# A fused transformer block on one core: constants made by another engine, a product 4 ticks sooner

## The chip, the cores and the metric

The kernel runs on one core of a Trainium2 chip. The core has a matrix engine (TensorE, PE in the rows), a vector engine (VectorE, DVE), an activation engine (ScalarE, ACT), a general engine (GpSimd, POOL) and a queue engine that issues most transfers (SyncE, SP). Each runs its own instructions in the order in which they were written and waits on semaphores for the others. The metric is the device time of one execution in microseconds (us), lower is better.

## The reference

One layer for 256 tokens of width 1024, in float32. `norm` is the root-mean-square norm over a row with a gain:

```python
h = norm(x, norm_mix_g);  proj = h @ w_in                  # u | q | k | v, 512 columns each
q, k = rope(norm_per_head(q)), rope(norm_per_head(k))      # 8 heads of 64
attn = causal_softmax(q @ k.T / 8) @ v
pool = (window_means(u, 2, 4, 8, 16) - u) @ pool_w * pool_scale   # 4 groups of 128
x = x + concat(pool, attn) @ w_out
h, m = norm(x, norm_xattn_g), norm(mem, norm_mem_g)        # mem: 256 x 1024
x = x + cross_attention(h @ w_xq, m @ w_xkv) @ w_xo        # 4 heads of 256, q and k normed
h = norm(x, norm_ffn_g)
up = causal_conv3(h @ w_up) + conv_b                       # 5632 columns: gate | val
x = x + (silu(gate) * val) @ w_down
```

The sequence is one block of 256 positions, so the attention over selected blocks comes to plain causal attention.

## The kernel before, in words

Weights stream from memory in chunks of 1 MB, each two units of 128x1024. Three buffers hold raw chunks (tile `raw`). For every unit ScalarE rounds it to a short format (`wh`, line 194) and VectorE makes what the rounding lost (`wl`, line 205); a product is then three matmuls: high by high, low by high, high by low. A raw buffer takes its next chunk only when both of its units have been through both engines. `need(u)` issues these two steps some units ahead of the one that TensorE takes up.

The order of work is written out by hand. TensorE's main work is a chain of matrix products. `a_chunk` computes 256 rows by 512 columns in eight steps of six 512-column matmuls (lines 366, 367 and 370) over units `u0` to `u0+3`. The first four calls make k, q, v and u (units 0 to 15, two steps a unit). Units 16 and 17 are one chunk of small constants for the pool mixing. Units 18 to 25 serve the keys of the memory, and the output projection follows, tile by tile (`b_tile`, lines 265 to 267).

Everything else is done by jobs, Python generators that each issue a few instructions and then yield. `tick()` lets every living job go one yield further; `a_chunk` calls it twice a step. So four ticks are two steps, and the tables `WAIT_...` say how many ticks a job lets pass at each of its places. Since every engine works in order, these numbers fix the order on each queue, not only the earliest time. `finish(jobs)` calls `tick` until the jobs named have ended.

These jobs matter here:

- `row_stat("x")` computes the mean square of each row of x. ScalarE makes eight squares (the first into `accx`, line 297, the others `sqx`, line 300), GpSimd adds them up (seven adds, line 301), then `WAIT_STAT[1]` ticks pass, and TensorE multiplies `accx` by a column of ones (line 281). VectorE makes `vx` of it (284), GpSimd `ex` (289). The same function with "m" serves the memory rows, and it reads the same `WAIT_STAT[1]`.
- `rope_table` makes the rotary tables `ropek` and `ropeq` on GpSimd (line 382), out of `tab`, a table that a transfer brings.
- `qk_job("k")` rotates k on VectorE: `m1k` out of `ropek` (404), `m2k` (408), the sums of squares `ssk` (411) and `m1k` again (413). Then it waits until `ex` has been issued, makes the head scale (`hk` at line 243, `rs1y` at 226, then twelve small GpSimd steps, lines 228 to 231), scales `m1k` by it (431), and TensorE transposes it (438). ScalarE copies the result to `qkT` (442). `qk_job("q")` does the same for q with `m1q` and `m2q`, and its scale ends in `sp` and `sneg` (445, 446).
- `score_job` (attention) takes the maximum of the scores, `nbs` from it and `sneg` (530), and the exponentials.
- `late_constants` makes `identr` and the first part of `maskr` (387, 388), which the scores need (515).
- `pool_job` splits u into `uh` and `ul` (250, 256), mixes (621 to 624), multiplies by the pool weights and empties the two banks into `cat` (643). `WAIT_POOL[7]` is the wait after that, at its end (644).

Of the kernel before, what the change touches and what calls it, by code (L numbers as in the profile page):

```python
# [16 lines left out]
P = 128  # L17
# [20 lines left out]
FIRST = 4  # L38

WAIT_MEAN = [0]  # L40
WAIT_STAT = [2, 14, 8, 0, 0, 30]
WAIT_ROPE = [6, 6, 0]
WAIT_QK = [12, 12, 8, 25, 0, 2]
WAIT_V = [2, 10]
WAIT_MEM = [2, 2]
WAIT_SCORE = [5, 4, 0, 9, 1, 6]
WAIT_ATTN = [2, 6, 0]
WAIT_POOL = [1, 6, 0, 7, 1, 5, 2, 6, 1]
WAIT_KEY = [0, 4, 7, 2, 0, 13, 5]
WAIT_R1 = [0]  # L50
WAIT_X = [3, 0, 0, 0, 10, 0, 6, 13, 8]
# [17 lines left out]
T_ID, T_MASK = 0, 128  # L69
T_COS, T_SIN = 384, 512  # L70
T_GQ, T_GQS, T_GK, T_GKS = 640, 704, 768, 832
# [5 lines left out]
def block_kernel(ctx: ExitStack, tc: tile.TileContext, wpack: bass.AP, xpack: bass.AP, scal: bass.AP,  # L77
                 memT: bass.AP, table: bass.AP, out: bass.AP):
    nc = tc.nc
    pe, act, dve, pool = nc.tensor, nc.scalar, nc.vector, nc.gpsimd  # L80
# [15 lines left out]
    def t2(name, dtype=F32):  # L96
        return temps.tile([P, 512], dtype, name=name, tag="t2", bufs=19)

    def t1(name):
        return temps.tile([P, S], F32, name=name, tag="t1", bufs=8)  # L100
# [12 lines left out]
    def go(gen):  # L113

        job = [gen, True]
        jobs.append(job)
        step(job)
        return job
# [16 lines left out]
    def wait(n):  # L135
        for _ in range(n):
            yield
# [7 lines left out]
    resid = sc[:, C_X:C_X + KT * S].rearrange("p (k s) -> p k s", k=KT)  # L145
    tab = const.tile([P, T_COLS], F32, name="tab")
# [32 lines left out]
    maskr = const.tile([P, 6 * P], F32R, name="maskr")  # L179
# [42 lines left out]
    def rsqrt(x, n):  # L222

        cnt[0] += 1
        y, t = sm(f"rs{cnt[0]}y", n), sm(f"rs{cnt[0]}t", n)
        dve.tensor_scalar(y.bitcast(I32), x.bitcast(I32), -0.5, float(0x5F3759DF), op0=ALU.mult, op1=ALU.add)
        for _ in range(3):
            pool.tensor_tensor(t, y, y, op=ALU.mult)  # L228
            pool.tensor_tensor(t, t, x, op=ALU.mult)
            pool.tensor_scalar(t, t, -0.5, 1.5, op0=ALU.mult, op1=ALU.add)  # L230
            pool.tensor_tensor(y, t, y, op=ALU.mult)
        return y
# [13 lines left out]
    def part_h(h, src, scale=None):  # L246
        if scale is None:
            act.copy(h, src)
        else:
            act.activation(h, src, AF.Copy, scale=scale)  # L250

    def part_l(l, src, h, scale=None):
        if scale is None:
            dve.tensor_tensor(l, src, h.bitcast(F32), op=ALU.subtract)
        else:
            dve.scalar_tensor_tensor(l, src, scale, h.bitcast(F32), op0=ALU.mult, op1=ALU.subtract)  # L256
# [12 lines left out]
    def col(t, c):  # L269
        return t[:, c:c + 1]  # L270
# [6 lines left out]
    def row_mean(acc, name):  # L277

        b = bank()
        for tt in range(TT):  # L280
            pe.matmul(b[:, tt:tt + 1], acc[:, tt * P:(tt + 1) * P], ones, start=True, stop=True)
        yield from wait(WAIT_MEAN[0])
        v = sm("v" + name, TT)
        dve.tensor_scalar(v, b[:, 0:TT], 1.0 / D, EPS, op0=ALU.mult, op1=ALU.add)
        return v

    def times_eps(v, name):
        e = sm("e" + name, TT)
        pool.tensor_scalar(e, v, EPS, None, op0=ALU.mult)
        return e  # L290

    def row_stat(name, src, behind=None):
        yield from wait(WAIT_STAT[3 if name == "x" else 4])
        acc = t1("acc" + name)
        for k in range(KT):
            if k == 0:
                act.activation(acc, src(k), AF.Square)
            else:
                sq = t1(f"sq{name}{k}")
                act.activation(sq, src(k), AF.Square)  # L300
                pool.tensor_tensor(acc, sq, acc, op=ALU.add)
            yield from wait(WAIT_STAT[0])
        if behind:
            behind()
        yield from wait(WAIT_STAT[1])
        v = yield from row_mean(acc, name)
        rows["e" + name] = times_eps(v, name)
        yield from wait(WAIT_STAT[2 if name == "x" else 5])
        rows[name] = rsqrt(v, TT)
# [64 lines left out]
    ident = tab[:, T_ID:T_ID + P]  # L374
    identr = const.tile([P, P], F32R, name="identr")
# [3 lines left out]
    def rope_table(n, g, gs):  # L379
        t = const.tile([P, 2, TT, HD], F32, name="rope" + n)  # L380
        for j, (c, gg) in enumerate(((T_COS, g), (T_SIN, gs))):
            pool.tensor_tensor(t[:, j], tab[:, c:c + 2 * HD].rearrange("p (t d) -> p t d", t=TT),
                               tab[:, None, gg:gg + HD].to_broadcast([P, TT, HD]), op=ALU.mult)
        rope_t[n] = t

    def late_constants():
        pool.tensor_copy(identr, ident)
        pool.tensor_copy(maskr[:, 0:2 * P], tab[:, T_MASK:T_MASK + 2 * P])
        pool.tensor_tensor(ggx, sc[:, C_GXQ:C_GXQ + 2], sc[:, C_GXK:C_GXK + 2], op=ALU.mult)


# [59 lines left out]

    def stat_job():

        yield from row_stat("x", lambda k: resid[:, k], lambda: rope_table("q", T_GQ, T_GQS))
        late_constants()

    rope_table("k", T_GK, T_GKS)
    stat_x = go(stat_job())
    bk = [bank(), bank()]
    a_chunk(0, xgv, bk)  # L460
# [135 lines left out]
    def pool_job():  # L596
        yield from wait(WAIT_POOL[8])

        rct = [t2(f"rct{i}") for i in range(2)]
        for g, w in enumerate(WINDOWS):  # L600
            r = rct[g // 2][:, g % 2 * S:(g % 2 + 1) * S]
            pool.memset(r[:, 16:], 1.0 / w)
            pool.tensor_copy(r[:, 0:16], tab[:, T_CNT + 16 * g:T_CNT + 16 * g + 16])
        us = []
        for tt in range(TT):
            us.append((t2(f"uh{tt}", F32R), t2(f"ul{tt}", F32R)))
            part_h(us[tt][0], bu[tt], col(rows["x"], tt))
        yield from wait(WAIT_POOL[0])
        for tt in range(TT):
            part_l(us[tt][1], bu[tt], us[tt][0], col(rows["x"], tt))  # L610
        yield from wait(WAIT_POOL[1])
        bp = []
        for g2 in range(2):
            b = bank()
            for i in range(2):
                g = 2 * g2 + i
                o = b[:, i * S:(i + 1) * S].rearrange("p (a s) -> p a s", a=2)
                c = slice(g * P, (g + 1) * P)
                b0 = misc[g2][:, i * S:(i + 1) * S].rearrange("p (a s) -> p a s", a=2)
                b1 = maskr6[:, 0:g + 3:g + 2]  # L620
                pe.matmul(o, us[0][0][:, c], b0, start=True, stop=False)
                pe.matmul(o, us[0][1][:, c], b0, start=False, stop=False)
                pe.matmul(o, us[1][0][:, c], b1, start=False, stop=False)
                pe.matmul(o, us[1][1][:, c], b1, start=False, stop=True)
            yield from wait(WAIT_POOL[2])
            pf, ph, pl = t2(f"pf{g2}"), t2(f"poolh{g2}", F32R), t2(f"pooll{g2}", F32R)
            dve.tensor_tensor(pf, b, rct[g2], op=ALU.mult)
            yield from wait(WAIT_POOL[3])
            act.copy(ph, pf)
            yield from wait(WAIT_POOL[4])  # L630
            dve.tensor_tensor(pl, pf, ph.bitcast(F32), op=ALU.subtract)
            bp.append((ph, pl))
        yield from wait(WAIT_POOL[5])
        for g2 in range(2):
            b = bank()
            for i in range(2):
                g = 2 * g2 + i
                w = [misc[3][:, g * P:(g + 1) * P], misc["l"][:, g * P:(g + 1) * P]]
                three(b[:, i * S:(i + 1) * S], w, [t[:, i * S:(i + 1) * S] for t in bp[g2]], True, True)
            yield from wait(WAIT_POOL[6])  # L640
            for i in range(2):
                g = 2 * g2 + i
                evac_split(cat[0][:, g], cat[1][:, g], b[:, i * S:(i + 1) * S], col(sc, C_PS + g))
        yield from wait(WAIT_POOL[7])
# [402 lines left out]
```

## Time and profile before

| what | value |
|---|---|
| time, median of 3 runs | 394.69 us (394.58 to 394.85) |
| the profiled execution | 395.07 us |
| its span, first to last instruction | 393.3 us |
| PE busy | 387.0 us (98%) |
| DVE busy | 283.1 us (72%) |
| ACT busy | 231.5 us (59%) |
| POOL busy | 90.0 us (23%) |

The span leaves out 1.77 us of the execution's own time, before the first and after the last instruction. PE's busy share is near the whole span, so what delays PE in its order delays the end, unless PE would have had to wait later anyway.

### The profile page before, as it was taken

How to read it: one execution, taken by the hardware profiler on the slowest of the kernel's cores; microseconds unless marked ns; L12 is line 12 of the kernel's file. 1: busy time of each engine (PE TensorE's matmuls, PEld its weight loads, DVE VectorE, ACT ScalarE, POOL GpSimd, SP SyncE). 2: the span in 40 equal slices, each digit the busy share in tenths (PEclk: the TensorE clock that was granted, in tenths of full speed). 3: DMA queues.
4: the chain of work that ended last, by engine and by line, in shares of the span. 5: the costliest groups of instructions: out<-in, count | busy, mean ns of one | idle time of the engine just before them, and what ended most of it. 6: DMA issues, size and time to landing. Idle time of an engine off the chain costs nothing.

```text
span 393.3 us, 7301 instructions
## 1 busy us (share of the span) xinstructions
PE 387.0 (98%) x2898; PEld 367.2 (93%) x2898; DVE 283.1 (72%) x478; ACT 231.5 (59%) x421; POOL 90.0 (23%) x174
## 2 busy tenths in 40 slices
PE   8999999999999999999999999999999999999996
PEld 7878787889999998899999999999999999999996
DVE  4788989956876667857774999998877874543350
ACT  5775886957476556845555498765665576342300
POOL 0384883134441423001647300000000000000000
PEclk9999999999999999999999999999999999999999
DMA  8985372543336537242545226665465452455400
GB/s 273 422 342 207 119 304 72 166 190 108 109 107 222 208 107 262 76 198 107 202 143 197 105 108 227 243 249 177 176 213 180 161 197 108 135 227 176 173 21 19
DMA packets 12274, 69.22 MB, mean 176 GB/s; under 512 B 1360, under 2 KB 2768, under 8 KB 4688
## 3 DMA queue, kind: packets, MB, share of 16 engines
q1 hardware_dynamic: 11952, 68.24, 47.9%
q8 instruction: 22, 0.36, 0.4%
q10 hardware_dynamic: 288, 0.52, 0.4%
q14 instruction: 12, 0.10, 0.1%
HBM read 67.71 MB, written 1.05 MB: 175 GB/s over the span
## 4 chain that ended last, share of the span: by engine, by line
PE 80%; DVE 7%; DMA 5%; ACT 3%; POOL 2%; issue 2%; SPq 0%; DVEq 0%; POOLq 0%
PE bank L265 23%; PE bank L267 23%; PE bank L266 23%; DMA raw<-wpack 3%; PE bank L366 3%; PE bank L367 3%; PE bank L370 3%; DVE wl L205 2%; DMA sc<-xpack 1%; ACT wh L194 1%; DVE mg_l L256 1%; ACT sqx L300 0%; PE bank L677 0%; PE bank L795 0%; POOL rs3t L228 0%
## 5 line engine op out<-in xcount | busy, mean ns | idle before, releaser
L205 DVE TENSOR_TENSOR wl<-raw,wh 128x1024 fp32r<-128x1024 f32 (+1 forms) x126 | 150.3, 1209 | 5.4 <-ACT wh L194 5.3
L194 ACT CAST wh<-raw 128x1024 fp32r<-128x1024 f32 (+1 forms) x125 | 123.7, 1024 | 41.6 <-DMA raw<-wpack 41.0
L265 PE MATMUL bank<-hs_h,wh 128*128 128x256 f32 x288 | 81.5, 283 | 0.0
L266 PE MATMUL bank<-hs_l,wh 128*128 128x256 f32 x288 | 81.5, 283 | 0.0
L267 PE MATMUL bank<-hs_h,wl 128*128 128x256 f32 x288 | 81.5, 283 | 0.0
L265 PEld LDWEIGHTS bank<-hs_h,wh 128*128 128x128 f32 x288 | 55.3, 192 | 0.0
L266 PEld LDWEIGHTS bank<-hs_l,wh 128*128 128x128 f32 x288 | 55.3, 192 | 0.0
L267 PEld LDWEIGHTS bank<-hs_h,wl 128*128 128x128 f32 x288 | 55.3, 192 | 0.0
L265 PE MATMUL bank<-act_h,wh 128*128 128x256 f32 x176 | 49.8, 283 | 0.0
L266 PE MATMUL bank<-act_l,wh 128*128 128x256 f32 x176 | 49.8, 283 | 0.0
L267 PE MATMUL bank<-act_h,wl 128*128 128x256 f32 x176 | 49.8, 283 | 0.0
L903 DVE SCALAR_TENSOR_TENSOR y<-bank,sc,y 128x255 f32<-128x255 f32 (+1 forms) x72 | 29.8, 479 | 14.4 <-ACT y L896 14.4
L265 PE MATMUL bank<-h_h,wh 128*128 128x256 f32 x128 | 36.6, 286 | 0.0
L267 PE MATMUL bank<-h_h,wl 128*128 128x256 f32 x128 | 36.2, 283 | 0.0
L266 PE MATMUL bank<-h_l,wh 128*128 128x256 f32 x128 | 36.2, 283 | 0.0
L896 ACT ACTIVATE y<-bank,sc 128x256 f32<-128x256 f32 x36 | 18.3, 559 | 27.6 <-PE bank L267 27.6
L265 PEld LDWEIGHTS bank<-act_h,wh 128*128 128x128 f32 x176 | 33.8, 192 | 0.0
L266 PEld LDWEIGHTS bank<-act_l,wh 128*128 128x128 f32 x176 | 33.8, 192 | 0.0
L267 PEld LDWEIGHTS bank<-act_h,wl 128*128 128x128 f32 x176 | 33.8, 192 | 0.0
L946 DVE TENSOR_TENSOR o<-bank,sc 128x256 f32<-128x256 f32 x8 | 3.4, 425 | 35.2 <-PE bank L267 35.2
L366 PE MATMUL bank<-wh,mg_h 128*128 128x512 f32 x64 | 26.1, 408 | 0.0
L726 POOL TENSOR_TENSOR h_acc<-h_sq,h_acc 128x256 f32<-128x256 f32 x14 | 16.8, 1198 | 40.3 <-ACT h_sq L725 40.2
(244 smaller groups left out, 862.4 us busy)
## 6 DMA issues: line engine op xcount, KB each, us to landing
raw<-wpack SPq DMA_DIRECT2D x59, 1024.0 KB, 4.8
raw<-wpack SPq DMA_DIRECT2D x4, 512.0 KB, 7.7
mraw<-memT SPq DMA_DIRECT2D x4, 256.0 KB, 7.7
out<-o SPq DMA_DIRECT2D x8, 128.0 KB, 1.9
raw<-wpack ACTq DMA_DIRECT2D x2, 256.0 KB, 3.7
raw<-wpack SPq DMA_DIRECT2D x2, 256.0 KB, 4.7
sc<-xpack SPq DMA_DIRECT2D x1, 512.0 KB, 6.0
tab<-table SPq DMA_DIRECT2D x1, 480.0 KB, 9.7
```

What stands on the lines that cost most here:

```text
L194: copy(split[u][0][:, r], unit(u)[:, r])
L205: dve.tensor_tensor(l[:, r], unit(u)[:, r], h[:, r].bitcast(F32), op=ALU.subtract)
L256: dve.scalar_tensor_tensor(l, src, scale, h.bitcast(F32), op0=ALU.mult, op1=ALU.subtract)
L265: pe.matmul(o, stat[0], mov[0], start=start, stop=False)
L266: pe.matmul(o, stat[0], mov[1], start=False, stop=False)
L267: pe.matmul(o, stat[1], mov[0], start=False, stop=stop)
L366: pe.matmul(bk[tt], a[tt][0], wv[0], start=k == 0, stop=False)
L367: pe.matmul(bk[tt], a[tt][1], wv[0], start=False, stop=False)
L370: pe.matmul(bk[tt], a[tt][0], wv[1], start=False, stop=k == KT - 1)
L726: pool.tensor_tensor(acc, sq, acc, op=ALU.add)
L896: act.activation(y[:, g * S:(g + 1) * S], src[:, g * S:(g + 1) * S], AF.Identity, bias=col(sc, C_CB + f), scale=col(sc, C_CW + 2 * 2 * NFF ...
L903: dve.scalar_tensor_tensor(yy[:, j:], uu[:, :S - j], col(sc, C_CW + (2 - j) * 2 * NFF + f), yy[:, j:], op0=ALU.mult, op1=ALU.add)
```

## The change

`late_constants` issues `identr` and `maskr` on ScalarE and no longer on GpSimd. `ropek` is made behind the seven adds of x's squares on GpSimd and no longer ahead of them. `WAIT_STAT[1]` goes from 14 to 10: the product of the summed squares and the column of ones is issued 4 ticks earlier, for x and for the memory. `WAIT_POOL[7]` goes from 6 to 2.

```diff
-WAIT_STAT = [2, 14, 8, 0, 0, 30]
+WAIT_STAT = [2, 10, 8, 0, 0, 30]
...
-WAIT_POOL = [1, 6, 0, 7, 1, 5, 2, 6, 1]
+WAIT_POOL = [1, 6, 0, 7, 1, 5, 2, 2, 1]
...
     def late_constants():
-        pool.tensor_copy(identr, ident)
-        pool.tensor_copy(maskr[:, 0:2 * P], tab[:, T_MASK:T_MASK + 2 * P])
+        act.copy(identr, ident)
+        act.copy(maskr[:, 0:2 * P], tab[:, T_MASK:T_MASK + 2 * P])
...
     def stat_job():
 
-        yield from row_stat("x", lambda k: resid[:, k], lambda: rope_table("q", T_GQ, T_GQS))
+        def tables():
+            rope_table("k", T_GK, T_GKS)
+            rope_table("q", T_GQ, T_GQS)
+
+        yield from row_stat("x", lambda k: resid[:, k], tables)
         late_constants()
 
-    rope_table("k", T_GK, T_GKS)
     stat_x = go(stat_job())
```

On GpSimd, at the start of the program, this stands in the kernel before (names with a number are one buffer each, the `sqx` are the seven squares):

```order
L382 TENSOR_TENSOR ropek<-tab 128x128 x2
L301 TENSOR_TENSOR accx<-sqx_190,accx 128x256
L301 TENSOR_TENSOR accx<-sqx_199,accx 128x256
...
L301 TENSOR_TENSOR accx<-sqx_260,accx 128x256
L382 TENSOR_TENSOR ropeq<-tab 128x128 x2
L289 TENSOR_SCALAR ex<-vx 128x2
```

and this in the changed one:

```order
L301 TENSOR_TENSOR accx<-sqx_187,accx 128x256
L301 TENSOR_TENSOR accx<-sqx_196,accx 128x256
...
L301 TENSOR_TENSOR accx<-sqx_257,accx 128x256
L382 TENSOR_TENSOR ropek<-tab 128x128 x2
L382 TENSOR_TENSOR ropeq<-tab 128x128 x2
L289 TENSOR_SCALAR ex<-vx 128x2
```

The two products for `ropek` moved from ahead of the seven adds to behind them.

On TensorE, in the second call of `a_chunk` (`wh_226` is unit 7 here, `wh_201` and `wh_223` are units 6 and 7 of the changed kernel), the kernel before has

```order
L370 MATMUL bank_283<-wl_252,xg_h 128x512
L281 MATMUL bank_354<-ones,accx 128x1 x2
L366 MATMUL bank_282<-wh_226,xg_h 128x512
L367 MATMUL bank_282<-wh_226,xg_l 128x512
L366 MATMUL bank_283<-wh_226,xg_h 128x512
```

and the changed one

```order
L370 MATMUL bank_283<-wl_225,xg_h 128x512
L281 MATMUL bank_332<-ones,accx 128x1 x2
L366 MATMUL bank_282<-wh_201,xg_h 128x512
L367 MATMUL bank_282<-wh_201,xg_l 128x512
L366 MATMUL bank_283<-wh_201,xg_h 128x512
```

The two products stood ahead of the call's last step (the second of unit 7) and now stand two steps, or 12 matmuls, further ahead, before the second step of unit 6.

On VectorE, behind the rotation of k, the kernel before has (`wl_346`, `wl_399` and `wl_417` are the low parts of units 11, 12 and 13)

```order
L205 TENSOR_TENSOR wl_346<-raw_202,wh_322 128x1024
L284 TENSOR_SCALAR vx<-bank_354 128x2
L243 TENSOR_SCALAR hk<-ssk,ex 128x8 x2
L226 TENSOR_SCALAR rs1y<-hk 128x16
L404 TENSOR_TENSOR m1q_385<-bank_282,ropeq 128x512
L404 TENSOR_TENSOR m1q_390<-bank_283,ropeq 128x512
L205 TENSOR_TENSOR wl_399<-raw_248,wh_344 128x1024
L205 TENSOR_TENSOR wl_417<-raw_248,wh_397 128x1024
L226 TENSOR_SCALAR rs2y<-vx 128x2
L431 TENSOR_TENSOR m1k_272<-m1k_272,rs1y 128x512
```

and the changed one (`wl_371`, `wl_399` and `wl_437` are units 11, 12 and 13; `vx` now stands ahead of the last rotation steps)

```order
L243 TENSOR_SCALAR hk<-ssk,ex 128x8 x2
L226 TENSOR_SCALAR rs1y<-hk 128x16
L205 TENSOR_TENSOR wl_371<-raw_199,wh_322 128x1024
L404 TENSOR_TENSOR m1q_385<-bank_282,ropeq 128x512
L404 TENSOR_TENSOR m1q_390<-bank_283,ropeq 128x512
L205 TENSOR_TENSOR wl_399<-raw_245,wh_369 128x1024
L226 TENSOR_SCALAR rs2y<-vx 128x2
L431 TENSOR_TENSOR m1k_272<-m1k_272,rs1y 128x512
L431 TENSOR_TENSOR m1k_277<-m1k_277,rs1y 128x512
L205 TENSOR_TENSOR wl_437<-raw_245,wh_397 128x1024
```

The head scale of k moved ahead of unit 11's split, and unit 13's split moved behind the scaling of k, which waits for GpSimd.

## Rows read from the trace of the kernel before

**Rows 1.** The page, parts 1 and 2: PE's busy time, and its granted clock.

```profile
PE 387.0 (98%) x2898; PEld 367.2 (93%) x2898; DVE 283.1 (72%) x478; ACT 231.5 (59%) x421; POOL 90.0 (23%) x174
PEclk9999999999999999999999999999999999999999
```

**Rows 2.** Who waited for whom, PE: total us, times, longest us.

```profile
PE bank L265 <- DVE cat_l L256: 0.4, 1, 0.4
```

**Rows 3.** Timeline of POOL from 19 us: start, us, instruction, idle before.

```profile
19.94 3.08 POOL L301 TENSOR_TENSOR accx<-sqx,accx 128x256 f32<-128x256 f32 x2 [0.46 <-ACT sqx L300]
23.10 0.74 POOL L301 TENSOR_TENSOR accx<-sqx,accx 128x256 f32<-128x256 f32 x1
24.74 1.78 POOL L301 TENSOR_TENSOR accx<-sqx,accx 128x256 f32<-128x256 f32 x1
27.89 0.45 POOL L382 TENSOR_TENSOR ropeq<-tab 128x128 f32<-128x128 f32 x1
```

**Rows 4.** Timeline of ACT: the last square, and a later split.

```profile
22.51 0.41 ACT L300 ACTIVATE sqx<-sc 128x256 f32<-128x256 f32 x1
33.56 2.00 ACT L194 CAST wh<-raw 128x1024 fp32r<-128x1024 f32 x2 [1.22 <-DMA raw<-wpack]
```

**Rows 5.** Timeline of PE, 23 to 28 us.

```profile
23.39 0.39 PE L366 MATMUL bank<-wh,xg_h 128*128 128x512 f32 x1
...
24.75 0.39 PE L366 MATMUL bank<-wh,xg_h 128*128 128x512 f32 x1
...
26.58 0.61 PE L281 MATMUL bank<-ones,accx 128*128 128x1 f32 x4 [0.30 <-POOL accx L301]
27.05 0.48 PE L366 MATMUL bank<-wh,xg_h 128*128 128x512 f32 x1
```

**Rows 6.** Timeline of DVE, 23 to 41 us.

```profile
23.51 1.29 DVE L404 TENSOR_TENSOR m1k<-bank,ropek 128x512 f32<-128x512 f32 x2 [1.09 <-ACT sqk L403]
24.72 2.89 DVE L205 TENSOR_TENSOR wl<-raw,wh 128x1024 fp32r<-128x1024 f32 x2
28.86 1.21 DVE L205 TENSOR_TENSOR wl<-raw,wh 128x1024 fp32r<-128x1024 f32 x1
...
34.01 0.37 DVE L243 TENSOR_SCALAR hk<-ssk,ex 128x8 f32<-128x8 f32 x2 [0.35 <-POOL ex L289]
...
39.98 1.29 DVE L431 TENSOR_TENSOR m1k<-m1k,rs1y 128x512 f32<-128x512 f32 x2 [1.80 <-POOL rs1y L231]
```

**Rows 7.** Timeline of POOL: two of the twelve scale steps, then the constants.

```profile
34.97 0.22 POOL L229 TENSOR_TENSOR rs1t<-rs1t,hk 128x16 f32<-128x16 f32 x1
...
35.87 1.12 POOL L228 TENSOR_TENSOR rs1t<-rs1y 128x16 f32<-128x16 f32 x1
...
45.43 2.08 POOL L388 CAST maskr<-tab 128x256 fp32r<-128x256 f32 x1
```

**Rows 8.** Timeline of PE around the transposes of k.

```profile
39.40 0.39 PE L366 MATMUL bank<-wh,xg_h 128*128 128x512 f32 x1
...
40.76 1.28 PE L438 MATMUL bank<-tab,m1k 128*128 128x128 f32 x8
41.80 0.47 PE L366 MATMUL bank<-wh,xg_h 128*128 128x512 f32 x1
```

**Rows 9.** The chain in order of time, 38 us: start, us, what.

```profile
38.09 4.66 DMA raw<-wpack
```

**Rows 10.** Timeline of ACT: q's copies. They follow the unit that rows 9 bring.

```profile
46.65 1.07 ACT L442 COPY qkT<-bank 128x512 f32<-128x512 f32 x2 [0.90 <-PE bank L438]
```

**Rows 11.** Timeline of PE: the mixing of u.

```profile
60.56 0.39 PE L621 MATMUL bank<-misc,uh 128*128 128x256 f32 x1 [0.60 <-DVE ul L256]
...
60.90 0.28 PE L623 MATMUL bank<-maskr,uh 128*128 128x256 f32 x1
61.22 0.39 PE L624 MATMUL bank<-maskr,ul 128*128 128x256 f32 x1
```

**Rows 12.** Timeline of DVE, 57 us: the wait on q's scale.

```profile
57.07 0.68 DVE L530 TENSOR_TENSOR nbs<-mxs,sneg 128x4 f32<-128x4 f32 x1 [1.88 <-POOL sneg L446]
```

## The prediction

> **What bounds the kernel now.** I read the page first. PE is busy in 387.0 of 393.3 us, at full granted clock in all 40 slices [rows 1], so the end is PE's amount of work plus the few moments at which its order stalls. I then read the table of waits, the timelines of the four engines up to 62 us, which is where the change moves instructions, and the chain of waits. PE stalls at four places that concern the change. At 26.58 it waits 0.30 for `accx` [rows 5]. At 40.76 the eight transposes of k take 1.04 up to 41.80 [rows 8], some 0.25 more than their work, since the second half waits for the scaled k. At 60.56 it has waited 0.60 for `ul`, and between 60.90 and 61.22 some 0.2 more for its second half, as the matmuls there otherwise follow at 0.12 [rows 11]. At 90 us it waits 0.4 for a bank that `cat_l` must read [rows 2]. That makes 1.55 us, which is all the change can win. What it can lose has no such limit: every stall that is new counts in full unless one of the later ones shrinks for it.
>
> **The product of x's squares.** This is the main term. It is issued two steps sooner, before the step that starts at 23.39 instead of the one at 27.05 [rows 5]. So the question is when `accx` is ready. The seven GpSimd adds no longer stand behind the two products for `ropek`. But the third add waited for ScalarE already (0.46) and starts at 19.94 [rows 3]. Its square is made where it was, so taking `ropek` out of the way does not move the last five adds. The third and fourth last until 23.02, the fifth takes 0.74 from 23.10, the sixth the same, and the seventh starts at 24.74 [rows 3]. Only that one should change. It took 1.78, beside a VectorE split that began at 24.72 [rows 6]; the 0.74 adds ran while VectorE had no split. Now VectorE comes to `m1k` first, which needs `ropek`, and that now stands behind the seventh add. So VectorE waits, issues no split, and the add takes 0.74, to 25.48.
>
> [...]
>
> The product starts 0.06 after the add, as before (26.58 against 26.52), and takes 0.47 to the next step (26.58 to 27.05 [rows 5]): the step that stood at 23.39 starts at 26.01, so the place costs 2.62. Before, the next step started at 27.05 instead of at 26.11 (24.75 and one step of 1.36 [rows 5]): 0.94. PE is 1.68 late from here on. Bounds: the last square ends at 22.92 [rows 4] and five adds of 0.74 with gaps of 0.08 from 19.94 would end at 24.04, which makes it +0.24; an unchanged `accx` makes it +2.7. I take 1.68, as only the row of the seventh add has a reason to change.
>
> **VectorE behind `ropek`.** `ropek`'s first product takes 0.45 when no split runs beside it [rows 3], so it is there at 26.0 and `m1k` starts at 26.05 instead of 23.51 [rows 6]: everything behind it on VectorE is 2.54 late, the splits of units 8 to 10 first. Unit 8's split, first behind `m1k`, then ends at about 28.6 (26.05 + 1.29 + 1.21). TensorE wants it 0.9 into the step behind the one at 27.05, at 29.3, and is itself 1.68 late, so this is covered by about 2.4 us. Then it gets some back. The head scale of k now stands ahead of unit 11's split (1.21) and no longer finds `ex` missing (0.35 [rows 6]). `hk` starts at 34.01 + 2.54 - 1.21 - 0.35 = 35.0, 1.0 late. The twelve GpSimd steps behind it are slow only where a split runs beside them (1.12 against 0.22 [rows 7]). Before, two were slow; now unit 11's and unit 12's splits meet them, so again two. The scaling of k starts at 39.98 + 1.0 = 41.0 [rows 6], and its halves end at 41.6 and 42.25.
>
> **The transposes of k** now stand one step sooner, where unit 12's first step started at 39.40 [rows 8]. PE comes there at 39.40 + 1.68 = 41.1, waits for the first half to 41.65, works 0.4, waits for the second to 42.3, and is done at 42.7. They take 1.6 instead of 1.04, so PE is 2.25 late behind them. Bounds: 0 (the scale comes 0.6 sooner) to 1.4 (a third slow step, 0.9 more).
>
> **What it finds later.** The scale of q follows the same VectorE order and comes about 1 us late; `nbs` waited for it at 57.07 [rows 12]. `ul`, behind it, is then ready at about 60.5 + 1.0. PE arrives at 59.96 + 2.25 = 62.2 and no longer waits: the 0.6 and the 0.2 go, and what is late next is PE itself. 2.25 - 0.8 = 1.45. The 0.4 at 90 us I leave: the chain of waits leads into it from PE's own work between 60 and 75 us, so it should move along with PE.
>
> **The edits that cost nothing.** `identr` and `maskr` on ScalarE stand between the splits of units 13 and 14, where ScalarE idled 1.22 for a transfer [rows 4]; two casts of at most half a 128x1024 cast (1.0) each fit in. Without that cover they would delay the splits of units 14 and 15 by as much, which TensorE takes up only after the transposes of q. GpSimd loses the 2.08 of `maskr` [rows 7], so the adds for the memory come sooner and may leave the scale of q undisturbed, up to 1 us, but PE then arrives after `ul` in any case. The memory's product, also 4 ticks sooner, still comes after the last add by the timeline of before. `WAIT_POOL[7]` is the wait behind the emptying of both banks: it empties nothing sooner, it only ends the loop of ticks sooner, so ScalarE and VectorE do two splits ahead of the second key job's squares. No wait of PE's is there; bounds -0.4 (the wait at 90) to +0.5 (a split late behind the key scale), taken as 0.
>
> **The sum.** 1.68 + 0.57 - 0.8 = 1.45; the possible help for the scale of q and small gaps make me take 1.3. The profiled execution would come to 395.07 + 1.3 = 396.4. It lies 0.38 above the median of the three runs, so the median goes from 394.69 to 396.0.
>
> **The rivals.**
> - Absorbed (about 395.2). The scale of k comes 0.6 sooner, the transposes add nothing, and the wait at 90 us shrinks too: 1.68 - 0.8 - 0.4 = 0.5. For it speaks that `hk` is off by three terms of which each is small; against it that the chain into the wait at 90 us leads through PE.
> - Faster (about 393.9). All five adds run at 0.74, `accx` is ready at 24.04, PE loses 0.24, `ropek` is ready at 24.5, and k's scale, only 0.4 behind its split, comes 0.5 before its old time. The stalls at 60 and 90 us then vanish (1.2): -0.8 with the transposes at +0.15. It decides at the third and fourth add: the two need 3.08 now [rows 3], and neither ScalarE's squares nor the splits beside them move. That speaks against it.
> - Transfers (about 397.0). A raw buffer comes free only after its second unit's split. Unit 13's split moves behind the scaling of k and ends at about 43.4 instead of 38.07. The load that followed took 4.66 [rows 9] and would land at 48.1. ScalarE stands at its split (1.05) and two smaller steps (0.8), so q's copies begin at 49.95; PE would let them start at 46.65 + 2.25 = 48.9 [rows 10]. That is up to 1.05 more at the scores.
> [...]
>
> **How the numbers follow.** The forecast (395.5 to 396.8) gets 0.58, absorbed 0.20, faster 0.10, transfers 0.08, clock 0.04. About 0.2%, or 0.8 us, is what a measurement of this kernel can tell from no change; 395.5 is that border. So slower is 0.70, same 0.20, faster 0.10. The range from 394.9 to 397.1 leaves out the faster case and the ends of transfers and clock.
>
> **What would show it.** In the changed profile GpSimd's third add starts near 19.9 and the seventh ends near 25.5; PE shows a wait of about 2.1 us on `accx`, the longest of the kernel; `m1k` starts at about 26 with a wait for GpSimd; the transposes of k show a wait for VectorE; the wait for `ul` is gone; units 14 and 15 are split after the two casts with no wait of PE's. A seventh add that ends by 24.1 would make the forecast wrong at its first step, and so would a stall of 0.6 still there at `ul`, for then PE had not been late enough.

## The result, and the profile after

The changed kernel takes 397.04 us (median of 6 runs, 396.60 to 397.46); the kernel before, on the same chip, 394.92 us (6 runs, 394.58 to 395.40). The ratio is 1.0053, with a 95% interval of 1.0040 to 1.0066: 2.1 us slower. The profiled execution of the changed kernel is the fastest of its six, 396.60 us with a span of 394.8; against the profiled execution before (395.07, 393.3) that is 1.5 us more.

Parts 1 and 2 of the page after answer to [rows 1].

```profile
PE 387.9 (98%) x2898; PEld 368.0 (93%) x2898; DVE 282.0 (71%) x478; ACT 231.7 (59%) x423; POOL 85.5 (22%) x172
PEclk9999999999999999999999999999999999999999
```

PE does the same 2898 matmuls at the same granted clock. The two casts have gone from GpSimd to ScalarE. The rest of the difference is waiting. Who waited for whom, PE, after (total us, times, longest us):

```profile
PE bank L281 <- POOL accx L301: 1.2, 1, 1.2
...
PE bank L281 <- POOL h_acc L729: 0.4, 1, 0.4
...
PE bank L624 <- DVE ul L256: 0.2, 1, 0.2
```

The wait for `accx` is now the longest, the 0.4 of [rows 2] is there unchanged (at 91.20 below), the wait for `ul` [rows 11] is smaller and not gone, and the wait for `h_acc` is new. Lines behind 457 count 3 more than before.

Timeline of POOL after (start, us, instruction, idle before), to be held against [rows 3]:

```profile
19.31 5.50 POOL L301 TENSOR_TENSOR accx<-sqx,accx 128x256 f32<-128x256 f32 x5 [0.70 <-ACT sqx L300]
...
117.24 1.79 POOL L729 TENSOR_TENSOR h_acc<-h_sq,h_acc 128x256 f32<-128x256 f32 x1 [1.43 <-ACT h_sq L728]
```

The last five adds take 5.50 us in one piece and end at 24.81; before, they ended at 26.52. `ropek` follows from 24.77. Timeline of ACT after, the squares and the constants:

```profile
18.75 0.72 ACT L300 ACTIVATE sqx<-sc 128x256 f32<-128x256 f32 x2
...
31.86 0.31 ACT L387 CAST identr<-tab 128x128 fp32r<-128x128 f32 x1
32.06 0.42 ACT L388 CAST maskr<-tab 128x256 fp32r<-128x256 f32 x1
33.66 2.01 ACT L194 CAST wh<-raw 128x1024 fp32r<-128x1024 f32 x2 [1.18 <-DMA raw<-wpack]
```

The casts lie ahead of a wait for a transfer that still lasts 1.18, and the split behind them begins 0.10 later than in [rows 4]. Timeline of PE after; its first lines answer to [rows 5], then [rows 8] and [rows 11]:

```profile
24.86 0.60 PE L281 MATMUL bank<-ones,accx 128*128 128x1 f32 x4 [1.23 <-POOL accx L301]
...
28.14 0.39 PE L366 MATMUL bank<-wh,xg_h 128*128 128x512 f32 x1
...
40.38 1.21 PE L438 MATMUL bank<-tab,m1k 128*128 128x128 f32 x8
41.35 0.47 PE L366 MATMUL bank<-wh,xg_h 128*128 128x512 f32 x1
...
61.07 0.39 PE L624 MATMUL bank<-misc,uh 128*128 128x256 f32 x1 [0.22 <-DVE ul L256]
...
61.41 0.28 PE L626 MATMUL bank<-maskr,uh 128*128 128x256 f32 x1
61.73 0.39 PE L627 MATMUL bank<-maskr,ul 128*128 128x256 f32 x1
...
67.40 0.66 PE L549 MATMUL bank<-tab,p 128*128 128x128 f32 x4
...
91.20 0.39 PE L265 MATMUL bank<-cat_h,wh 128*128 128x256 f32 x1 [0.39 <-DVE cat_l L256]
...
119.09 0.61 PE L281 MATMUL bank<-ones,h_acc 128*128 128x1 f32 x4 [0.43 <-POOL h_acc L729]
119.56 0.63 PE L680 MATMUL bank<-tab,kn 128*128 128x128 f32 x4
119.94 0.36 PE L265 MATMUL bank<-h_h,wh 128*128 128x256 f32 x1
```

The same places of PE before:

```profile
66.22 0.60 PE L546 MATMUL bank<-tab,p 128*128 128x128 f32 x4
...
90.36 0.39 PE L265 MATMUL bank<-cat_h,wh 128*128 128x256 f32 x1 [0.39 <-DVE cat_l L256]
...
116.94 0.60 PE L677 MATMUL bank<-tab,kn 128*128 128x128 f32 x4
...
118.10 0.50 PE L281 MATMUL bank<-ones,h_acc 128*128 128x1 f32 x4
118.46 0.36 PE L265 MATMUL bank<-h_h,wh 128*128 128x256 f32 x1
```

and the last add of GpSimd for that product:

```profile
116.40 0.75 POOL L726 TENSOR_TENSOR h_acc<-h_sq,h_acc 128x256 f32<-128x256 f32 x1 [1.13 <-ACT h_sq L725]
```

And DVE after, for [rows 6]:

```profile
25.25 1.29 DVE L404 TENSOR_TENSOR m1k<-bank,ropek 128x512 f32<-128x512 f32 x2 [3.46 <-POOL ropek L382]
26.46 2.35 DVE L205 TENSOR_TENSOR wl<-raw,wh 128x1024 fp32r<-128x1024 f32 x2
...
33.65 0.36 DVE L243 TENSOR_SCALAR hk<-ssk,ex 128x8 f32<-128x8 f32 x2
...
39.58 1.30 DVE L431 TENSOR_TENSOR m1k<-m1k,rs1y 128x512 f32<-128x512 f32 x2 [1.80 <-POOL rs1y L231]
...
41.93 1.41 DVE L408 TENSOR_TENSOR m2q<-bank,ropeq 128x256 f32<-128x256 f32 x4
...
60.27 1.40 DVE L256 SCALAR_TENSOR_TENSOR ul<-bank,rs2y,uh 128x512 fp32r<-128x512 f32 x2
...
66.65 0.69 DVE L630 TENSOR_TENSOR pf<-bank,rct 128x512 f32<-128x512 f32 x1
```

with three lines of DVE before that rows 6 do not have:

```profile
41.19 1.41 DVE L408 TENSOR_TENSOR m2q<-bank,ropeq 128x256 f32<-128x256 f32 x4
...
59.77 1.40 DVE L256 SCALAR_TENSOR_TENSOR ul<-bank,rs2y,uh 128x512 fp32r<-128x512 f32 x2
...
66.14 0.69 DVE L627 TENSOR_TENSOR pf<-bank,rct 128x512 f32<-128x512 f32 x1
```

Behind the wait for `accx` PE is 1.09 late (28.14 against 27.05 [rows 5]), but that lateness does not last as such. Followed along PE, what lasts comes in at three places:

- **At the mixing of u: +0.51** (61.07 against 60.56). `ul` starts 0.50 later than before (60.27 against 59.77). `m1k` waited 3.46 us for `ropek` and started 1.74 late; from there to `ul` VectorE needs 35.02 us instead of 36.26. The scaling of k is even 0.40 early (39.58 against 39.98 [rows 6]), because the head scale of k no longer stands behind a split, the two splits behind `m1k` are shorter and the wait for `ex` is gone. But unit 13's split now stands behind that scaling, so `m2q` is 0.74 late (41.93 against 41.19), and only 0.24 of it is made good up to `ul`: 0.50.
- **Between there and the wait for `cat_l`: +0.33** (91.20 - 61.07 = 30.13, before 29.80). The memory's product, 4 ticks sooner, takes its bank sooner (at 63.82, before at 68.05), and the transposes of p now take a bank that `pf` has just emptied: they start at 67.40, and `pf` ends at 66.65 + 0.69 = 67.34. Before, they started at 66.22, ahead of the end of `pf` (66.14 + 0.69).
- **At 119 us: +0.64** (119.94 against 118.46 is 1.48, of which 0.84 was there at `cat_l`). `WAIT_POOL[7]` has shifted the second key job. Before, four transposes of `kn` stood ahead of the product of `h_acc`, and the last add took 0.75, from 116.40. Now the product stands first, the last add takes 1.79, and PE waits 0.43.

Together 1.48 of the 1.5 us between the two spans.

The 0.51 flatters the change. ScalarE's squares stand behind a split that waits for a transfer, and in this execution that split began at 17.80, before at 18.43; so the third add of the squares starts at 19.31 instead of 19.94 [rows 3]. Counted from that add, PE comes to the mixing of u after 41.76 us (19.31 to 61.07) and before after 40.62 (19.94 to 60.56 [rows 11]): the stage costs 1.14. With 0.33 and 0.64 that makes 2.11, what the medians show.

### The profile page after: what moved, and what is told of

It is laid out like the page before. It is cut to its first block, busy times and chain, and to the rows that moved or that the text cites. A ratio compares the mean times of both kernels' runs of the same rounds, so it can differ in the third digit from the quotient of the medians.

```text
span 394.8 us, 7300 instructions
## 1 busy us (share of the span) xinstructions
PE 387.9 (98%) x2898; PEld 368.0 (93%) x2898; DVE 282.0 (71%) x478; ACT 231.7 (59%) x423; POOL 85.5 (22%) x172
## 4 chain that ended last, share of the span: by engine, by line
PE 85%; DVE 4%; ACT 4%; DMA 3%; POOL 2%; issue 1%; SPq 0%; ACTq 0%; POOLq 0%
PE bank L265 23%; PE bank L267 23%; PE bank L266 23%; PE bank L366 5%; PE bank L367 5%; PE bank L370 5%; DMA raw<-wpack 2%; DVE wl L205 1%; DMA sc<-xpack 1%; ACT wh L194 1%; PE bank L438 0%; PE bank L680 0%; POOL h_acc L729 0%; PE bank L798 0%; ACT sqx L300 0%
## 5 line engine op out<-in xcount | busy, mean ns | idle before, releaser
L729 POOL TENSOR_TENSOR h_acc<-h_sq,h_acc 128x256 f32<-128x256 f32 x14 | 17.8, 1273 | 41.2 <-ACT h_sq L728 41.1
```

## The experiments

All were timed in five rounds beside the kernel before, on three chips in turn; its medians there were 395.14 (first four runs), 394.92 (next four) and 394.97 (last two). **Theory 1** is the prediction's: the wait for `accx` makes PE late, and it stays late. **Theory 2** is the one read from the trace: VectorE is late behind `ropek`, so `ul` is late; what PE waits for `accx` only replaces what it would wait for `ul`.

| run | edit | ratio to before, 95% interval | median |
|---|---|---|---|
| after | the change | 1.0053 (1.0040 to 1.0066) | 397.04 |
| u_pool | `WAIT_POOL[7]` undone | 1.0043 (1.0025 to 1.0060) | 396.62 |
| u_rope | `ropek` first again | 1.0096 (1.0072 to 1.0119) | 398.86 |
| u_stat | products 4 ticks later again | 1.0065 (1.0050 to 1.0080) | 397.94 |
| u_mask | constants on GpSimd again | 1.0057 (1.0039 to 1.0075) | 397.47 |
| sq6 | squares 1 tick apart | 1.0026 (1.0014 to 1.0038) | 395.77 |
| pm | constants and `WAIT_POOL[7]` alone | 1.0023 (1.0013 to 1.0033) | 395.99 |
| stat8 | products 2 ticks sooner still | 1.0089 (1.0063 to 1.0115) | 398.53 |
| stat12 | products 2 ticks later | 1.0055 (1.0039 to 1.0071) | 396.96 |
| e_m | memory's product and `WAIT_POOL[7]` undone | 1.0035 (1.0023 to 1.0047) | 396.43 |
| v1 | `ropek` on VectorE, see below | 0.9979 (0.9965 to 0.9992) | 394.14 |

**u_pool.**

```diff
-WAIT_POOL = [1, 6, 0, 7, 1, 5, 2, 2, 1]
+WAIT_POOL = [1, 6, 0, 7, 1, 5, 2, 6, 1]
```

> The changed kernel with WAIT_POOL[7] back at 6. Theory (the shift of the second key job costs): its last transposes stand again ahead of the product of the summed squares of h, cover the last GpSimd add, the wait of 0.4 at 119 us goes, and the time falls by 0.5 to 0.6, to about 396.4. Rival (that wait is absorbed, and the setting does nothing, as predicted): 397.0.

396.62, 0.4 under the changed kernel and on another chip; the intervals overlap. In its trace the wait for `h_acc` is gone, and the transposes of `kn` (118.39) stand ahead of the product (119.55) again. Here ScalarE's squares start at 19.40 and not at 18.75, and `ul` at 60.90: the squares' place differs between executions by some 0.65 us, and everything up to `ul` follows. The third add:

```profile
19.95 5.50 POOL L301 TENSOR_TENSOR accx<-sqx,accx 128x256 f32<-128x256 f32 x5 [0.74 <-ACT sqx L300]
```

and PE:

```profile
25.51 0.61 PE L281 MATMUL bank<-ones,accx 128*128 128x1 f32 x4 [1.51 <-POOL accx L301]
...
61.70 0.39 PE L624 MATMUL bank<-misc,uh 128*128 128x256 f32 x1 [0.20 <-DVE ul L256]
```

With the third add where it was before (19.94 [rows 3]), the mixing of u is 1.14 late (60.56 before). From that add it is 41.75 us, as in the changed kernel's profile (41.76).

**u_rope.** The products for `ropek` stand ahead of the adds again.

```diff
-            rope_table("k", T_GK, T_GKS)
...
+    rope_table("k", T_GK, T_GKS)
     stat_x = go(stat_job())
```

> The changed kernel with ropek again ahead of the seven adds. accx is then ready at about 26.5 while its product stands 2 steps sooner: TensorE waits some 3 us for it, but m1k starts on time at 23.5. Theory 1 (TensorE's lateness behind accx decides, as predicted): 2.7 late there, 0.8 absorbed at ul: 397.3 to 397.8. Theory 2 (VectorE's lateness behind ropek decides, since TensorE still waits for ul in the changed trace, and the wait for accx is absorbed): the scale of q is on time, 396.0 or less.

398.86, slower than the whole change and above both figures; theory 2's (396.0 or less) missed by 2.9. Part of it is a cause that neither theory had at its centre. Windows of this trace (us, then the busy time and count of PE, PEld, DVE, ACT and POOL, then PEclk, DMA share, GB/s):

```profile
24.00:26.00 2.00, 0.16 (x1) 0.00 (x0) 2.00 (x3) 0.26 (x1) 1.92 (x3) 1.00 1.07 451
28.00:30.00 2.00, 2.00 (x6) 1.53 (x5) 2.00 (x5) 1.55 (x2) 0.23 (x1) 0.50 0.79 262
32.00:34.00 2.00, 2.00 (x11) 1.64 (x10) 1.97 (x6) 1.69 (x3) 1.34 (x2) 1.00 0.04 16
```

PE's timeline in the same trace, at the end of the wait and in the slow stretch:

```profile
26.07 0.61 PE L281 MATMUL bank<-ones,accx 128*128 128x1 f32 x4 [1.91 <-POOL accx L301]
...
28.30 0.63 PE L366 MATMUL bank<-wh,xg_h 128*128 128x512 f32 x1
28.73 0.63 PE L367 MATMUL bank<-wh,xg_l 128*128 128x512 f32 x1
```

PE stands 1.91 us for `accx`; then, while it works again without a gap, the granted clock of a stretch (28 to 30 us) is 0.50, and matmuls follow at 0.43. `m1k` starts at 22.94 and `ul` at 59.39, so VectorE is not late, yet PE is: it comes to the mixing of u at 63.39 and finds `ul` there. Where VectorE is on time, PE's own lateness counts, as theory 1 has it. One step of six matmuls there took 2.56 us (28.30 to 30.86), against 1.36 in the kernel before, at full clock (23.39 to 24.75 [rows 5]). All six runs show a mean clock of 0.991 to 0.996.

**u_stat.** `WAIT_STAT[1]` is 14 again, with `ropek` still behind the adds.

```diff
-WAIT_STAT = [2, 10, 8, 0, 0, 30]
+WAIT_STAT = [2, 14, 8, 0, 0, 30]
```

> The changed kernel with WAIT_STAT[1] back at 14. The wait for accx goes. Theory 1 (that wait decides): 395.8. Theory 2 (VectorE's lateness decides): the head scale of k stands behind one more split again and comes 1.4 later than in the changed kernel, ul comes no sooner, and the time stays, 396.7 to 397.2.

397.94, above what either theory gave: taking the wait for `accx` away does not help, and the time rises. The scaling of k, behind one more split again, starts at 41.52 (39.58 in the changed kernel), and PE waits for it, in the waits of this trace:

```profile
PE bank L438 <- DVE m1k L431: 1.7, 1, 1.7
```

The transposes start at 42.27, and the lower clock shows in the stretch behind them (0.50 from 44 to 46 us). It does not explain the time: the three executions at a mean clock of 0.994 took 397.69 to 397.84, the three at full clock 398.03 to 398.35.

**u_mask.** `late_constants` on GpSimd again.

```diff
-        act.copy(identr, ident)
-        act.copy(maskr[:, 0:2 * P], tab[:, T_MASK:T_MASK + 2 * P])
+        pool.tensor_copy(identr, ident)
+        pool.tensor_copy(maskr[:, 0:2 * P], tab[:, T_MASK:T_MASK + 2 * P])
```

> The changed kernel with identr and maskr made by GpSimd again. Theory 2 (the scale of q decides): GpSimd's adds for the memory come 2.4 later and again lie beside the steps of VectorE ahead of q's scale, so ul comes 0.5 to 0.7 later: 397.6. Theory 1 (TensorE is late anyway): 397.0, no change.

397.47, the same as the changed kernel within both intervals. Its three runs at full clock lie at 396.90, 396.97 and 397.31, as the changed kernel's do; its three others, at a mean clock of about 0.996, at 397.63 to 398.70. Moving the constants costs and gains nothing that can be measured.

**sq6.** x's squares follow one tick apart, the product stays in the place that the change gave it, and `WAIT_POOL[7]` is 6.

```diff
-            yield from wait(WAIT_STAT[0])
+            yield from wait(1 if name == "x" else WAIT_STAT[0])
...
-        yield from wait(WAIT_STAT[1])
+        yield from wait(18 if name == "x" else WAIT_STAT[1])
```

> The changed kernel with the squares of x issued one tick apart instead of two (product and tables stay where they are) and WAIT_POOL[7] back at 6. The last squares then fall into ScalarE's idle time before its third split and GpSimd's adds end about 2 us sooner, near 23. Theory (the wait for accx, and ropek behind it, are the loss): no wait at the product, m1k at about 24, no wait for ul: 393.5 to 394.3, below the kernel before. Rival (the loss is elsewhere, in the new order of VectorE): 396 or more.

395.77, a miss for both figures: it lost 1.3 of the 2.1 us but was not faster than before. It keeps the memory's product 4 ticks sooner. POOL's timeline in this trace:

```profile
16.14 8.26 POOL L301 TENSOR_TENSOR accx<-sqx,accx 128x256 f32<-128x256 f32 x7 [15.72 <-ACT sqx L300]
```

and DVE's:

```profile
24.86 1.29 DVE L404 TENSOR_TENSOR m1k<-bank,ropek 128x512 f32<-128x512 f32 x2 [2.67 <-POOL ropek L382]
```

With the squares early, the seven adds run without a pause, and they still take 8.26 us. The wait for `accx` falls to 0.29, but `ropek` stands behind the adds, and `m1k` waits 2.67 for it.

**pm.** The changed kernel with `WAIT_STAT[1]` at 14 and `ropek` first (the edits of u_stat and u_rope): only the constants and `WAIT_POOL[7]` are left of the change.

> Of the change only identr and maskr on ScalarE and WAIT_POOL[7] at 2. Theory (the loss is the wait for accx with ropek behind it, plus 0.5 at 119 us for the shift of the key job): 395.5, the wait of 0.4 for h_acc there and nothing new ahead of 90 us. Rival (the constants on ScalarE cost, too): 396 or more.

395.99, 1.07 over the kernel before (0.5 to 1.3 by the interval). Its trace has the wait for `h_acc` (0.43), and the last add takes 1.79 there as well. The third add of x's squares and the mixing of u there:

```profile
19.34 6.58 POOL L301 TENSOR_TENSOR accx<-sqx,accx 128x256 f32<-128x256 f32 x5 [0.30 <-ACT sqx L300]
```

and

```profile
59.92 0.38 PE L624 MATMUL bank<-misc,uh 128*128 128x256 f32 x1 [0.29 <-DVE ul L256]
```

In this profiled execution, the fastest of its eleven, the mixing of u begins 0.64 sooner than before. That is the squares again, and not a gain from the constants: from the third add it is 40.58 us, before 40.62. The new wait gives the 0.64 back by 118.46, so the span is that of before, 393.3. As u_mask puts no price on the constants, the loss by medians is put down to `WAIT_POOL[7]`; that its size is 1.07 and not the 0.64 of the trace is not shown, and u_pool's 0.4 is lower.

**stat8 and stat12.** `WAIT_STAT[1]` alone, at 8 and at 12.

```diff
-WAIT_STAT = [2, 10, 8, 0, 0, 30]
+WAIT_STAT = [2, 8, 8, 0, 0, 30]     # stat8; 12 in stat12
```

> The changed kernel with WAIT_STAT[1] at 8: the product stands one more step sooner. TensorE waits 1.36 longer for accx, some 3 us. Theory 1 (that wait counts, and the lower clock that two traces show behind waits of 1.5 to 1.9 costs some 1.5 more): 398.5 to 400, granted clock below 0.997 in most executions. Theory 2 (the wait is absorbed by the later one for ul): 397.0.

> The changed kernel with WAIT_STAT[1] at 12: the product stands one step later. The wait for accx falls from about 1.5 to 0.2, and the granted clock stays at 1. Theory 1 (that wait and the clock behind it count): 396.0 to 396.4. Theory 2 (absorbed; VectorE's lateness behind ropek decides): 396.8 to 397.1.

stat12 decides between the theories for the changed order. It has no wait for `accx` left, and takes 396.96 where the change takes 397.04. (The profiled execution took 398.20, the slowest of the six, but its span, 395.2, is within the others', 394.9 to 395.4.) PE's timeline in its trace:

```profile
40.75 1.21 PE L438 MATMUL bank<-tab,m1k 128*128 128x128 f32 x8 [1.15 <-issue]
```

and the mixing of u:

```profile
61.44 0.39 PE L624 MATMUL bank<-misc,uh 128*128 128x256 f32 x1 [0.22 <-DVE ul L256]
```

The 1.2 us that PE no longer stands at 24 us it stands ahead of the transposes of k, whose input `m1k` VectorE scales from 39.96 on, and it meets `ul` with the same 0.2 to wait. From the third add (19.65) to the mixing it is 41.79 us, in the changed kernel 41.76. That is theory 2. In stat8 the wait for `accx` grows to 2.87; its two runs at full clock take 396.90 and 397.33, no more than the changed kernel, and the four others, at 0.990 to 0.996, 398.47 to 400.57. So by these two a longer stall there costs nothing by itself either, until the clock falls behind it; the median, 398.53, is the one that theory 1 gave with its price for the clock.

**e_m.** `WAIT_POOL[7]` at 6, and the memory's product back at 14 ticks; x's stays at 10.

```diff
-        yield from wait(WAIT_STAT[1])
+        yield from wait(WAIT_STAT[1] if name == "x" else 14)
```

> The changed kernel with the memory's product back in its place (14 ticks for the memory, 10 for x) and WAIT_POOL[7] at 6, so ropek behind the adds, x's product 4 ticks sooner and the constants on ScalarE are left. Theory (three separate losses: ul 0.5 late by VectorE's lateness behind ropek, 0.3 at 67 us where the moved product of the memory shifts the turn of the banks, 0.6 at 119 us): the last two go, 396.1, and the wait of TensorE for pf at 67 us is not there. Rival (the 0.3 is lateness of VectorE too): 396.5, as with WAIT_POOL[7] undone alone.

396.43. From the mixing of u to the wait for `cat_l` it takes 29.83 (29.80 before, 30.13 after), and the transposes of p are ahead of the end of `pf` again:

```profile
66.92 0.60 PE L549 MATMUL bank<-tab,p 128*128 128x128 f32 x4
```

Its span, 394.0, is 0.7 over that of before, and its mixing of u is 0.70 late (61.26): with both edits undone nothing else is left in the trace. The third add starts at 19.50 here, so from it to the mixing it is 41.76 us again, 1.14 more than before. The median is 1.46 over before's; the rest is not explained.

**v1**, a version made from what the runs showed. VectorE makes `ropek` while it waits for transfers, the squares come as in sq6, x's product stands where the change put it, plus two ticks, and the two late edits are undone.

```diff
-    def rope_table(n, g, gs):
+    def rope_table(n, g, gs, eng=pool):
...
-        yield from wait(WAIT_STAT[1])
+        yield from wait(20 if name == "x" else 14)
...
+    def rope_k_job():
+        yield from wait(5)
+        rope_table("k", T_GK, T_GKS, dve)
+        yield
...
+    go(rope_k_job())
```

> A version against both: ropek made by VectorE in its idle time behind unit 5's split, x's squares one tick apart, x's product 2 ticks sooner than before, the memory's product and WAIT_POOL[7] as before, the constants on ScalarE. Theory (the loss is that m1k waits for ropek behind the adds; the sooner head scale of k by itself gains 1.2 on VectorE): m1k starts right behind sqk, ul comes 1.2 sooner than before, TensorE no longer waits for it, 393.5 to 394.0. Rival (TensorE's order gives nothing back): 394.9 or more.

394.14, ratio 0.9979 (0.9965 to 0.9992): faster than both, if by 0.8 us only. DVE's timeline in its trace:

```profile
17.11 1.03 DVE L382 TENSOR_TENSOR ropek<-tab 128x128 f32<-128x128 f32 x2
...
22.50 1.29 DVE L404 TENSOR_TENSOR m1k<-bank,ropek 128x512 f32<-128x512 f32 x2 [0.18 <-ACT sqk L403]
...
58.07 1.40 DVE L256 SCALAR_TENSOR_TENSOR ul<-bank,rs2y,uh 128x512 fp32r<-128x512 f32 x2
```

and PE's:

```profile
59.91 0.28 PE L626 MATMUL bank<-misc,uh 128*128 128x256 f32 x1
```

With neither the adds ahead of `ropek` nor `ropek` ahead of the adds, `ul` comes 1.70 sooner than before (0.32 of it because the transfer ahead of the squares came sooner), and PE does not wait for it; a wait of 0.49 for `accx` is left at 25.56.

## Why the prediction came out as it did

The sign held, and the first cause it named (GpSimd's two jobs in a new order) is that of the stage up to 62 us. That 397.04 lies within its range (394.9 to 397.1, by 0.06, and outside the 395.5 to 396.8 that it thought likeliest) is in part luck. Counted from the third add, the stage cost 1.14 where the sum had 1.45, and 0.97 came from two edits that it had costed at nothing.

**The adds.** The prediction had the last five take 5.54 us (19.94 to 25.48), with the seventh at 0.74 because VectorE waits for `ropek`. They took 5.50, the last two 1.53 together. In the profiled execution they began 0.63 sooner, as ScalarE's squares did, so the wait for `accx` was 1.23, against 2.1, and PE 1.09 late. In u_pool, where the squares stood as before, the product starts at 25.51 (25.54 predicted) and PE is 1.74 late behind it (28.79 against 27.05; 1.68 predicted): this step was right. That an add is long beside a split and short without one was the prediction's reading of two lengths in the rows (1.78 and 0.74). The short seventh add here, with no split between 21.79 and 26.46, and the long last one of `h_acc` (1.79, beside a split from 117.23) fit it; no run shows why it is so.

**VectorE and the transposes of k, +0.57.** This term was wrong: the transposes took 0.97 instead of 1.04, with no wait. `m1k` did wait and was 1.74 late (2.54 predicted, the difference being mostly the earlier adds), but `hk` was 0.36 early instead of 1.0 late. Besides the split and the wait for `ex`, which the prediction took off, the two splits behind `m1k` took 2.35 instead of 2.89 [rows 6]; the adds, which before ran beside them to 26.52, had ended at 24.81.

**The wait for `ul`, -0.8: the step that failed.** "PE arrives at 59.96 + 2.25 = 62.2 and no longer waits" held neither in the changed kernel (arrival at 60.85, a wait of 0.22, and 0.32 between the last two lines of the mixing, where the others follow at 0.12) nor in u_pool, e_m or stat12. The prediction had `ul` about 1.0 late, and in u_pool it is 1.13 late (60.90 against 59.77); but it followed PE's lateness, which the 0.57 had made too large, and took `ul` to be covered by it. In fact `ul` set the time, and PE's stall was absorbed ahead of it: stat12 removes that stall and gains nothing. The stage is worth `ul`'s lateness, 1.14 from the third add on, and not 1.45.

**The edits costed at nothing.** For the constants on ScalarE that was right (u_mask). For the memory's product it was wrong by 0.33 (29.83 in e_m against 30.13), through the order in which banks come round; the prediction asked only whether the last add was done. For `WAIT_POOL[7]` it was wrong by 0.64 in the trace (0.4 by the medians of u_pool, 1.07 by those of pm): the prediction looked for its effect at the wait at 90 us and at a late split, and it lies at 119, where the second key job ends up behind the product of `h_acc`.

**The stalls before.** The five that the prediction lists add up to 1.75, not 1.55; its sum does not use the figure.

**The rivals.** The 0.04 for the clock, and its end beyond the range, rest on no row: before, the clock is full in all 40 slices [rows 1]. The profiled executions of u_rope, u_mask, u_stat and stat8 show a lower one (means of 0.996, 0.996, 0.994 and 0.996; 0.50 in a stretch of u_rope and of u_stat) behind stalls of 1.91, 1.5, 1.73 and 2.87 us. It does not decide the result: the profile of the changed kernel is at full clock in all slices, and the two of its executions with the lowest mean clock, 0.994, took 396.95 and 397.25, and the one at full clock beside the profiled one 397.09. The transfers rival shows on ScalarE, which waits 1.95 for a load (by the prediction's reckoning the one behind unit 13's split) and starts q's copies at 48.60, not at 46.65 [rows 10]; but PE has no wait at the scores. Absorbed was right in that the scale of k came sooner and the transposes added nothing, but the wait at 90 us did not shrink; that its 0.5 is also the 0.51 of the trace is the luck of the earlier squares.

**Open.** That the squares' place makes the difference between 1.5 us (the profiles) and 2.1 (the medians) fits the profiles of the changed kernel, u_pool, e_m, stat12 and pm, but where the squares began in the executions without a profile is not known. e_m's median is 0.3 more than its trace shows, and pm's 0.4 more.

## What to carry to other kernels

Where two engines are late at a common meeting point, their delays don't add: follow both to that point and take the later, and test it by removing one. A wait at the end of a job in a program ordered by hand is an edit to everything that the job's end releases, so walk the order to the end of the program, the turns of buffers and banks included, before costing it at nothing. Before two profiles are compared place by place, line them up at an event that the change does not move, as the third add here; without that, 0.6 us of an earlier transfer passed for a smaller loss. Where a reorder on one engine trades one late result for another, look for a third engine that idles (v1).

## What the runs showed of the hardware

The granted clock fell while PE was already working again: in u_rope the wait of 1.91 us ends at 26.07, and the slow matmuls are those from about 28 us on (a clock of 0.50 from 28 to 30 us); from 32 to 34 us it is 1.00 again. Behind waits of 1.2 to 1.5 us one profiled execution shows it (u_mask, at 1.5: a mean of 0.996) and three don't (after, u_pool, e_m: 1.000, 0.999 and 1.000). It comes in part of the executions, so the profile of one may miss it: stat8 takes 396.90 us at full clock and 400.57 at a mean of 0.990 with one and the same order. A mean below 1 is not always a longer time: e_m takes 396.41 to 396.69 at 0.995 and 0.996, and 396.36 and 396.65 at full clock.

An add on GpSimd took longer beside a split of VectorE's: 1.78 us before (the split from 24.72) and 1.79 after (from 117.23), against 0.74 with no split beside it (23.10 [rows 3]). The same seven adds, without a pause between them, take 8.26 us in sq6 and 9.36 in v1, where `ropek` and the first splits behind `m1k` run on VectorE beside them. Bringing their inputs sooner therefore won less than I expected of sq6.
